# Seven half-block products in place of eight: three quarters of each MLP's second product by Strassen's scheme

## Chip, cores and metric

One core of a Trainium2 chip runs the whole kernel as one program. The metric is the device time of one execution in microseconds. The engines are named as the profile names them: PE is TensorE's matmul, DVE is VectorE, ACT is ScalarE, POOL is GpSimd, SP is the engine whose queue issues the DMAs.

## What is computed

The reference is a two-layer encoder on 512 tokens of width 1024, all in float32: layer 0 has windowed and neighbourhood attention, layer 1 a bidirectional state-space scan. Each layer ends in the same MLP with a squared relu:

```python
def squared_relu_mlp(x, w1, w2):
    return jnp.square(jax.nn.relu(x @ w1)) @ w2
...
x = layer_norm(DN_ALPHA * x + mix, ln1_g[i], ln1_b[i])
x = layer_norm(DN_ALPHA * x + squared_relu_mlp(x, mlp_w1[i], mlp_w2[i]), ln2_g[i], ln2_b[i])
```

`w1` is 1024 x 4096 and `w2` is 4096 x 1024. The change touches the product with `w2`.

## The kernel before

Every large product is done with operands split in two: `hi` is the value rounded to the matmul's fp32r type, `lo` the rest, and `split3` (line 215) adds three matmuls, hi x hi, hi x lo and lo x hi. A full matmul has 512 columns and contracts 128 rows.

**Weights.** `Weights` (line 42) walks a list of chunks of 128 x 1024 values in the order of their use. `prepare` loads a chunk by SP (line 73, tile `w_raw`), makes `w_hi` on ACT (line 74) and `w_lo` on DVE, or on POOL for the chunks that `ON_POOL` lists (line 75). `next` keeps three chunks ahead of the one that it returns. The pool "w" has four buffers of each tile; `widen` (line 84) adds a second pool "w2" with four more, and then four chunks in turn come from "w2" and four from "w".

**The MLP** (`Main.mlp`, line 416) works in four quarters of 1024 hidden values. In a quarter the first product makes eight tiles of 128 hidden values x 512 tokens (`project`, 24 matmuls a chunk), and `act` makes relu and square on ACT, the square again in fp32 and its low half on DVE. The second product (`sweep`, line 281) goes over two halves of 512 output columns. In each, eight k-tiles meet four groups of 128 tokens, in four PSUM banks: 4 chunks x 24 matmuls. So a quarter has 192 + 192 matmuls. `drain` (line 321) adds a bank to the residual rows `res` on DVE. The last quarter's second half is followed by the layer norm and by transposes; the first quarter's first four tiles run as half-width pieces (`first_tiles`).

**Order.** PE's order is as written; in the MLP quarters the instructions of ACT, DVE, POOL and SP are ordered by a scheduler when the program is built, and each engine then works strictly in that order.

Of the kernel before, what the change touches and what calls it, by code (L numbers as in the profile page):

```python
# [9 lines left out]
F32 = mybir.dt.float32  # L10
# [17 lines left out]
G = 8  # L28
# [13 lines left out]
class Weights:  # L42


    def __init__(self, nc, pool, sources, ahead, in_order):
        self.in_order = in_order
        self.nc = nc
        self.pools = [pool]
# [4 lines left out]
        self.wide_from = self.wide_until = 0  # L53
        self.at = 0

    def prepare(self, after=(), between=None):
# [3 lines left out]
        src = self.sources[self.at]  # L60
        wide = self.wide_from <= self.at < self.wide_until and (self.at - self.wide_from) % (4 + self.extra) < self.extra
        pool = self.pools[1 if wide else 0]
        self.at += 1
        n = src.shape[1]
        raw = pool.tile([P, 1024], F32, name="w_raw")
# [5 lines left out]
        eng = nc.gpsimd if self.at - 1 in ON_POOL else nc.vector  # L71
        for cols in (slice(0, n),) if between is None else (slice(0, n // 2), slice(n // 2, n)):
            nc.sync.dma_start(out=raw[:, cols], in_=src[:, cols])
# [9 lines left out]

    def widen(self, pool, extra, n):


        self.extra = extra
        self.pools = [self.pools[0], pool]
        self.wide_from = self.at + 4 - len(self.ready)
        self.wide_until = self.at - len(self.ready) + n  # L90
# [28 lines left out]
def tile_encoder_trunk(ctx: ExitStack, tc: tile.TileContext, a: dict, out: bass.AP, stop=None):  # L119
# [36 lines left out]
    for q in range(4):  # L156
        sources += [a["w_m1"][0, q * 8 + i] for i in range(8)]
        sources += [a["w_m2"][0, q, i] for i in range(8)]
    sources += [a["w_dt"]]
    sources += [a["w_ssm"][i] for i in range(6 * G)]  # L160
    sources += [a["w_so"][i] for i in range(16)]
    for q in range(4):
        sources += [a["w_m1"][1, q * 8 + i] for i in range(8)]
        sources += [a["w_m2"][1, q, i] for i in range(8)]
# [92 lines left out]
    class Main:  # L257
# [10 lines left out]
        def more_weights(self, bufs, n):  # L268
            self.w2_ctx = tc.tile_pool(name="w2", bufs=bufs)
            weights.widen(self.w2_ctx.__enter__(), bufs, n)  # L270

        def fewer_weights(self):
            self.w2_ctx.__exit__(None, None, None)

# [141 lines left out]
        def mlp(self, layer, ends):  # L416
            xh, xl = rows_of(self.xT[0]), rows_of(self.xT[1])
            hh, hl = rows_of(self.h_slots.hi()), rows_of(self.h_slots.lo())
# [9 lines left out]
            for q in range(4):  # L428
                first = 0
                if q == 0:  # L430
                    first = 4
                    for i, ps in enumerate(self.first_tiles(first)):
                        act(ps, i)
                for i in range(first, 8):
                    ps = mm_bank()
                    project(ps, weights.next(), xh, xl)
                    act(ps, i)
                if q == 3:
                    self.load_ln(2 * layer + 1)
# [959 lines left out]
```

## Time and profile before

| | us |
|---|---|
| median of three runs | 1416.11 (1415.49 to 1420.14) |
| the profiled execution | 1418.63 |
| its span, first to last instruction | 1416.8 |
| PE busy | 1386.0 (98%) |
| DVE busy | 837.8 (59%) |
| ACT busy | 619.6 (44%) |
| POOL busy | 356.5 (25%) |

The page gives for each engine the time in which an instruction of it was in work. A time in which an instruction of DVE or POOL is held up after it has started counts as busy too. Matmuls are pipelined, so their busy times overlap and pace is read from their starts, or from what each finished tile releases.

### The profile page before, as it was taken

How to read it: one execution, taken by the hardware profiler on the slowest of the kernel's cores; microseconds unless marked ns; L12 is line 12 of the kernel's file. 1: busy time of each engine (PE TensorE's matmuls, PEld its weight loads, DVE VectorE, ACT ScalarE, POOL GpSimd, SP SyncE). 2: the span in 40 equal slices, each digit the busy share in tenths (PEclk: the TensorE clock that was granted, in tenths of full speed). 3: DMA queues.
4: the chain of work that ended last, by engine and by line, in shares of the span. 5: the costliest groups of instructions: out<-in, count | busy, mean ns of one | idle time of the engine just before them, and what ended most of it. 6: DMA issues, size and time to landing. Idle time of an engine off the chain costs nothing.

```text
span 1416.8 us, 18694 instructions
## 1 busy us (share of the span) xinstructions
PE 1386.0 (98%) x7104; PEld 1142.2 (81%) x7104; DVE 837.8 (59%) x1222; ACT 619.6 (44%) x1105; POOL 356.5 (25%) x248
## 2 busy tenths in 40 slices
PE   8999999999999999998999999999999999999997
PEld 7777779888888888986888788878888888888886
DVE  4577559434344343869789788887586243443426
ACT  5688725314133140357766567664324133231320
POOL 1255310000000020216664657665213000000000
PEclk9999999999999999999999999999999999999999
DMA  8232255333333230245454454532544233232101
GB/s 295 79 124 64 68 196 176 105 93 101 90 105 90 86 100 30 100 129 154 144 151 132 132 154 145 156 101 77 198 152 161 77 110 98 89 104 75 60 0 60
DMA packets 62401, 161.48 MB, mean 114 GB/s; under 512 B 9612, under 2 KB 19624, under 8 KB 62312
## 3 DMA queue, kind: packets, MB, share of 16 engines
q1 hardware_dynamic: 62312, 160.29, 36.4%
q8 instruction: 56, 0.92, 0.3%
q14 instruction: 33, 0.27, 0.1%
HBM read 154.87 MB, written 5.39 MB: 113 GB/s over the span
## 4 chain that ended last, share of the span: by engine, by line
PE 81%; DVE 6%; POOL 4%; DMA 3%; issue 2%; ACT 1%; SPq 1%; DVEq 0%; POOLq 0%; ACTq 0%
PE mm L216 19%; PE mm L217 19%; PE mm L218 19%; PE b L217 5%; PE b L218 5%; PE b L216 5%; POOL tb L947 1%; POOL e L956 1%; DVE xs L843 1%; PE y L1099 1%; SPq L548 1%; DVE w_lo L75 1%; PE y L1110 1%; PE o L635 1%; DMA r<-ac_d 1%
## 5 line engine op out<-in xcount | busy, mean ns | idle before, releaser
L74 ACT ACTIVATE w_hi<-w_raw 128x1024 fp32r<-128x1024 f32 (+1 forms) x216 | 225.8, 1052 | 462.7 <-PE mm L217 201.8
L216 PE MATMUL mm<-hi,w_hi 128*128 128x512 f32 (+1 forms) x1048 | 412.9, 394 | 0.0
L75 DVE TENSOR_TENSOR w_lo<-w_raw,w_hi 128x1024 fp32r<-128x1024 f32 (+1 forms) x185 | 254.0, 1377 | 252.3 <-ACT w_hi L74 251.5
L217 PE MATMUL mm<-lo,w_hi 128*128 128x512 f32 (+1 forms) x1048 | 398.5, 380 | 0.0
L218 PE MATMUL mm<-hi,w_lo 128*128 128x512 f32 (+1 forms) x1048 | 397.4, 379 | 0.0
L216 PEld LDWEIGHTS mm<-hi,w_hi 128*128 128x128 f32 x1048 | 197.1, 188 | 40.4 <-issue 5.5
L218 PEld LDWEIGHTS mm<-hi,w_lo 128*128 128x128 f32 x1048 | 196.9, 188 | 39.2
L217 PEld LDWEIGHTS mm<-lo,w_hi 128*128 128x128 f32 x1048 | 197.6, 189 | 33.0
L75 POOL TENSOR_TENSOR w_lo<-w_raw,w_hi 128x1024 fp32r<-128x1024 f32 (+1 forms) x31 | 76.7, 2479 | 411.5 <-ACT w_hi L74 411.5
L216 PE MATMUL mm<-w_hi,hi 128*128 128x512 f32 x352 | 141.2, 401 | 5.7 <-ACT hi L178 5.0
L218 PE MATMUL mm<-w_hi,lo 128*128 128x512 f32 x352 | 138.9, 394 | 0.0
L217 PE MATMUL mm<-w_lo,hi 128*128 128x512 f32 x352 | 138.8, 394 | 0.0
L217 PE MATMUL b<-w_lo,hi 128*128 128x512 f32 (+1 forms) x328 | 123.5, 377 | 1.6 <-DVE w_lo L75 1.6
L216 PE MATMUL b<-w_hi,hi 128*128 128x512 f32 (+1 forms) x328 | 123.6, 377 | 0.0
L218 PE MATMUL b<-w_hi,lo 128*128 128x512 f32 (+1 forms) x328 | 123.4, 376 | 0.0
L370 POOL TENSOR_TENSOR rstd<-ve,half 128x1 f32<-128x1 f32 x16 | 13.1, 819 | 358.8 <-DVE neg L368 339.6
L947 POOL TENSOR_TENSOR tb<-r,dmask 128x1024 f32<-128x1024 f32 x32 | 83.7, 2626 | 31.3 <-DMA r<-ac_d 30.1
L951 ACT ACTIVATE tb<-tb,ac_tok 128x128 f32<-128x128 f32 x256 | 80.6, 390 | 22.5 <-POOL tb L947 22.5
L216 PEld LDWEIGHTS mm<-w_hi,hi 128*128 128x128 f32 x352 | 66.7, 189 | 20.9 <-ACT hi L178 5.0
L218 PEld LDWEIGHTS mm<-w_hi,lo 128*128 128x128 f32 x352 | 66.5, 189 | 15.5 <-DVE lo L239 0.4
L217 PEld LDWEIGHTS mm<-w_lo,hi 128*128 128x128 f32 x352 | 66.7, 189 | 13.8
L425 DVE TENSOR_TENSOR sq<-relu 128x512 f32<-128x512 f32 x64 | 60.5, 948 | 24.4 <-ACT relu L423 24.4
(287 smaller groups left out, 1883.8 us busy)
## 6 DMA issues: line engine op xcount, KB each, us to landing
w_raw<-in_w_m_dram SPq DMA_DIRECT2D x128, 512.0 KB, 3.6
w_raw<-in_w_ssm_dram SPq DMA_DIRECT2D x48, 512.0 KB, 3.6
r<-ac_d SPq DMA_DIRECT2D x64, 256.0 KB, 4.6
w_raw<-in_w_so_dram SPq DMA_DIRECT2D x16, 512.0 KB, 3.7
w_raw<-in_w_att_dram SPq DMA_DIRECT2D x14, 512.0 KB, 5.8
r<-ac_d SPq DMA_DIRECT2D x64, 96.0 KB, 2.9
w_raw<-in_w_ao_dram SPq DMA_DIRECT2D x8, 512.0 KB, 3.6
xraw<-in_xT_dram SPq DMA_DIRECT2D x8, 256.0 KB, 6.4
```

The costliest lines, as they stand in the source:

```text
L74: split = [nc.scalar.activation(hi[:, cols], raw[:, cols], AF.Copy), eng.tensor_tensor(lo[:, cols], raw[:, cols], hi[:, cols].bitcast(F32) ...
L75: eng.tensor_tensor(lo[:, cols], raw[:, cols], hi[:, cols].bitcast(F32), op=ALU.subtract)]
L216: PE.matmul(ps, lhs_h, rhs_h, start=first, stop=False)
L217: PE.matmul(ps, lhs_h, rhs_l, start=False, stop=False)
L218: PE.matmul(ps, lhs_l, rhs_h, start=False, stop=last)
L425: DVE.tensor_tensor(s, r, r, op=ALU.mult)
L548: nc.sync.dma_start(out=vj[r * 32:r * 32 + 32, j, kt, :], in_=vb_g[kt * 4 + r, NA_START[j]:NA_START[j] + 32, pair * P:pair * P + P])
L635: PE.matmul(o_ps[64 * e:64 * e + 64, self.n * P:self.n * P + P], va[:, b, kv:kv + 64], self.pt[e][:, i * P:i * P + P], start=(i == 0), sto ...
L843: DVE.scalar_tensor_tensor(acc[:, lo_o:lo_o + n], ps[:, lo_i:lo_i + n], cw[:, i, k:k + 1], acc[:, lo_o:lo_o + n], op0=ALU.mult, op1=ALU.add)
L947: POOL.tensor_tensor(v["x"], v["r"].rearrange("p d (c l) -> p d c l", c=NT), bc(dmask.unsqueeze(2), [P, 2, NT, P]), op=ALU.add)
L951: pin(ACT.activation(v["x"][:, d, c, :], v["x"][:, d, c, :], AF.Exp, bias=ac_tok[:, c, 32 * d + hf:32 * d + hf + 1]))
L956: POOL.tensor_tensor(es[g, h], v["x"][:, 0], v["x"][:, 1], op=ALU.add)
```

## The change

In the quarters 0, 1 and 2 of both layers the second product is done by blocks. The quarter's hidden values are a 2 x 2 block matrix H (512 tokens as two halves of 256, 1024 hidden values as two halves of 512), the weights a 2 x 2 block matrix W of 512 x 512 blocks. Seven products of block sums replace the eight products of blocks. Each has 24 matmuls in two PSUM banks.

- Sums of H blocks are made by DVE in the fp32 tile `s` and split again into four slots of the `hi` and `lo` tiles.
- Sums of W blocks are made by POOL (`less`), in fp32, in the eight raw tiles `w2r` of a quarter and two tiles `t1`. The chunk list then has 14 entries for such a quarter; of their low halves DVE makes eleven, POOL those of the entries 7, 10 and 13.
- One product goes into two places of `res` (two pairs of DVE additions from PSUM). One product is copied by ACT to `u`; two others are added to it by DVE, and POOL adds `u` to `res`.
- `w_raw` has three buffers instead of four. The pool "w2" holds raw blocks and is no longer a source of `w_hi` and `w_lo`, save for four chunks at a time that are lent at the ends of two sweeps of layer 0.

```diff
-        raw = pool.tile([P, 1024], F32, name="w_raw")
+        made = callable(src)
+        raw = src() if made else pool.tile([P, 1024], F32, name="w_raw", bufs=3)
...
-        eng = nc.gpsimd if self.at - 1 in ON_POOL else nc.vector
+        eng = nc.gpsimd if on_pool else nc.vector
...
+        def less(to, x, y, p):
+            nc.gpsimd.tensor_tensor(v[to, p], v[x, p], v[y, p], op=ALU.subtract)
+        def get(b, p, *sums):
+            def make():
+                if not v:
+                    for i, name in enumerate(("11", "21", "12", "22")):
+                        for j in range(2):
+                            v[name, j] = blocks["pool"].tile([P, 1024], F32, name="w2r")
+                            nc.sync.dma_start(out=v[name, j], in_=a["w_m2"][layer, q, 2 * i + j])
+                    for j in range(2):
+                        v["T1", j] = blocks["pool"].tile([P, 1024], F32, name="t1", bufs=2)
+                        less("T1", "12", "11", j)
+                        less("12", "22", "12", j)
+                for args in sums:
+                    less(*args, p)
+                return v[b, p]
+            return make
+        for b, *sums in (("11",), ("21", ("11", "22", "T1")), ("T1", ("21", "21", "11")), ("22",), ("11",), ("12",), ("21",)):
+            chunks += [get(b, p, *sums) for p in range(2)]
...
+                sources.extend((c, i in (7, 10, 13)) for i, c in enumerate(sums))
...
+        def act(self, ps, i):
...
+            if i in (5, 7):
...
+                DVE.tensor_tensor(h22, h21, h22, op=ALU.add)
+                DVE.tensor_tensor(h21, h11, h21, op=ALU.subtract)
+                DVE.tensor_tensor(h11, h22, h11, op=ALU.subtract)
+                DVE.tensor_tensor(h12, h12, h11, op=ALU.subtract)
+            if i == 7:
+                self.split(3, self.s[:, 1, :, 256:])
...
+        def product(self, o):
+            banks = [mm_bank() for _ in range(2)]
+            for p in range(2):
+                wh, wl = weights.next()
+                for kk in range(2):
+                    k = 2 * p + kk
+                    for t in range(2):
+                        ts = slice(t * P, t * P + P)
+                        cs = slice(kk * 512, kk * 512 + 512)
+                        split3(banks[t], self.hi[:, o, k, ts], self.lo[:, o, k, ts], wh[:, cs], wl[:, cs],
+                               k == 0, k == 3)
...
+        def products(self, scale):
+            x = self.product(0)
+            self.split(0, s[:, 1, :, :256])
+            for t in range(2):
+                ACT.activation(u[t], x[t], AF.Copy)
+            self.add(x, 0, 0, scale)
+            x = self.product(1)
+            self.split(1, s[:, 0, :, :256])
+            self.add(x, 0, 0)
+            x = self.product(3)
+            self.split(3, s[:, 0, :, 256:])
+            self.add(x, 1, 1, scale)
+            self.add(x, 0, 1, scale)
+            self.add(self.product(0), 0, 1)
+            x = self.product(1)
+            for t in range(2):
+                DVE.tensor_tensor(u[t], u[t], x[t], op=ALU.add)
+            self.add_u(u, 0, 1)
+            x = self.product(3)
...
+            self.add_u(u, 1, 1)
+            self.add(self.product(2), 1, 0, scale)
+            self.add_u(u, 1, 0)
```

The built orders show what this moves. DVE in the second product of layer 0's first quarter, before (`w_lo` is a chunk's low half, `res` with `mm` or `b` an addition from PSUM), and now, from chunk 4 (`t1`) to the activation splits of the slots 0 and 1 (`lo<-s,hi`; `s<-s` are sums):

```order
L75 TENSOR_TENSOR w_lo_3250<-w_raw_3248,w_hi_3249 128x1024
L75 TENSOR_TENSOR w_lo_3281<-w_raw_3279,w_hi_3280 128x1024
L75 TENSOR_TENSOR w_lo_3312<-w_raw_3310,w_hi_3311 128x1024
L323 SCALAR_TENSOR_TENSOR res0_2383<-res0_2383,mm_3085 128x512
L323 SCALAR_TENSOR_TENSOR res1_2384<-res1_2384,mm_3086 128x512
L323 SCALAR_TENSOR_TENSOR res2_2385<-res2_2385,mm_3087 128x512
L323 SCALAR_TENSOR_TENSOR res3_2386<-res3_2386,mm_3088 128x512
L75 TENSOR_TENSOR w_lo_3343<-w_raw_3341,w_hi_3342 128x1024
```

```order
L75 TENSOR_TENSOR w_lo_3131<-t1_2990,w_hi_3130 128x1024
L534 TENSOR_TENSOR s_2672<-s_2672 128x2x256
L278 TENSOR_TENSOR lo_2674<-s_2672,hi_2673 128x1024
L370 SCALAR_TENSOR_TENSOR res0_2383<-res0_2383,mm_3110 128x512
L535 TENSOR_TENSOR s_2672<-s_2672 128x2x256
L370 SCALAR_TENSOR_TENSOR res1_2384<-res1_2384,mm_3111 128x512
L75 TENSOR_TENSOR w_lo_3156<-t1_2993,w_hi_3155 128x1024
L536 TENSOR_TENSOR s_2672<-s_2672 128x2x256
L75 TENSOR_TENSOR w_lo_3172<-w2r_2986,w_hi_3171 128x1024
L372 TENSOR_TENSOR res0_2383<-res0_2383,mm_3152 128x512
L372 TENSOR_TENSOR res1_2384<-res1_2384,mm_3153 128x512
L278 TENSOR_TENSOR lo_2674<-s_2672,hi_2673 128x1024 x2
```

The splits of block sums and the additions of each product now alternate with the weight splits, where eight additions stood in two groups.

POOL after layer 0's first layer norm, before, and now at the end of the first quarter's second product, from chunk 7 to chunk 13 (`t1` is a block sum of the next quarter, `res` with `sq` the addition of `u`):

```order
L370 TENSOR_TENSOR rstd_2654<-ve_2651,half_75 128x1
L75 TENSOR_TENSOR w_lo_3529<-w_raw_3527,w_hi_3528 128x1024
L75 TENSOR_TENSOR w_lo_4522<-w_raw_4520,w_hi_4521 128x1024
L75 TENSOR_TENSOR w_lo_4633<-w_raw_4631,w_hi_4632 128x1024
L75 TENSOR_TENSOR w_lo_4781<-w_raw_4779,w_hi_4780 128x1024
```

```order
L75 TENSOR_TENSOR w_lo_3194<-w2r_2988,w_hi_3193 128x1024
L75 TENSOR_TENSOR w_lo_3250<-w2r_2982,w_hi_3249 128x1024
L162 TENSOR_TENSOR t1_3587<-w2r_3579,w2r_3571 128x1024
L563 TENSOR_TENSOR res0_2383<-res0_2383,sq_3108 128x512
L162 TENSOR_TENSOR t1_3590<-w2r_3581,w2r_3573 128x1024
L563 TENSOR_TENSOR res1_2384<-res1_2384,sq_3109 128x512
L75 TENSOR_TENSOR w_lo_3308<-w2r_2980,w_hi_3307 128x1024
```

POOL had six full splits in the whole MLP of layer 0. Now two block sums of the next quarter and two additions stand ahead of chunk 13's split.

SP at the same place, before, and now (the blocks of the second quarter; `w2r_3577` takes the buffer of chunk 9, `w2r_3579` that of chunk 10, `w2r_3581` that of chunk 11):

```order
L73 DMA w_raw_3217<-in_w_m2_dram 128x1024
L73 DMA w_raw_3248<-in_w_m1_dram 128x1024
L73 DMA w_raw_3279<-in_w_m1_dram 128x1024
L73 DMA w_raw_3310<-in_w_m1_dram 128x1024
L73 DMA w_raw_3341<-in_w_m1_dram 128x1024
```

```order
L170 DMA w2r_3575<-in_w_m2_dram 128x1024
L170 DMA w2r_3577<-in_w_m2_dram 128x1024
L170 DMA w2r_3579<-in_w_m2_dram 128x1024
L170 DMA w2r_3581<-in_w_m2_dram 128x1024
L170 DMA w2r_3583<-in_w_m2_dram 128x1024
L73 DMA w_raw_3391<-in_w_m1_dram 128x1024
L73 DMA w_raw_3427<-in_w_m1_dram 128x1024
L170 DMA w2r_3585<-in_w_m2_dram 128x1024
```

The loads of the next quarter's blocks stand in one run, each behind the release of a buffer by this quarter's splits.

## Rows read from the trace of the kernel before

**Rows 1.** The page: busy time, share of the span, instructions.
```profile
PE 1386.0 (98%) x7104; PEld 1142.2 (81%) x7104; DVE 837.8 (59%) x1222; ACT 619.6 (44%) x1105; POOL 356.5 (25%) x248
```

**Rows 2.** Windows, layer 0's third quarter: us, then busy per engine, PEclk, DMA.
```profile
core 0: us, PE busy (x) PEld busy (x) DVE busy (x) ACT busy (x) POOL busy (x), PEclk, DMA share, GB/s
408.60:497.10 88.50, 88.50 (x385) 72.16 (x385) 35.00 (x39) 25.95 (x33) 2.40 (x1) 1.00 0.31 94
```

**Rows 3.** Timeline of ACT in that quarter: start us, us, instruction [idle before <-releaser].
```profile
408.67 0.58 ACT L423 ACTIVATE relu<-mm 128x512 f32<-128x512 f32 x1
414.27 0.58 ACT L423 ACTIVATE relu<-mm 128x512 f32<-128x512 f32 x1
...
430.95 0.58 ACT L423 ACTIVATE relu<-mm 128x512 f32<-128x512 f32 x1
...
436.39 0.58 ACT L423 ACTIVATE relu<-mm 128x512 f32<-128x512 f32 x1
...
457.77 1.06 ACT L74 ACTIVATE w_hi<-w_raw 128x1024 fp32r<-128x1024 f32 x1 [4.57 <-PE mm L218]
463.39 1.06 ACT L74 ACTIVATE w_hi<-w_raw 128x1024 fp32r<-128x1024 f32 x1 [4.56 <-PE mm L218]
```

**Rows 4.** Timelines of DVE and POOL: durations of undisturbed operations.
```profile
1061.49 2.41 DVE L75 TENSOR_TENSOR w_lo<-w_raw,w_hi 128x1024 fp32r<-128x1024 f32 x2 [0.54 <-ACT w_hi L74]
...
1079.26 1.29 DVE L426 TENSOR_TENSOR lo<-sq,hi 128x512 fp32r<-128x512 f32 x2
...
1118.40 2.05 DVE L323 SCALAR_TENSOR_TENSOR res<-res,mm 128x512 f32<-128x512 f32 x3 [1.08 <-PE mm L218]
...
695.87 1.29 POOL L956 TENSOR_TENSOR e<-tb 128x512 f32<-128x512 f32 x1
...
519.59 2.40 POOL L75 TENSOR_TENSOR w_lo<-w_raw,w_hi 128x1024 fp32r<-128x1024 f32 x1 [19.81 <-ACT w_hi L74]
```

**Rows 5.** The same timelines where DVE and POOL have work at once.
```profile
515.20 0.68 DVE L425 TENSOR_TENSOR sq<-relu 128x512 f32<-128x512 f32 x1
...
520.03 2.50 DVE L425 TENSOR_TENSOR sq<-relu 128x512 f32<-128x512 f32 x1 [3.34 <-ACT relu L423]
...
580.13 5.72 POOL L75 TENSOR_TENSOR w_lo<-w_raw,w_hi 128x1024 fp32r<-128x1024 f32 x2 [2.24 <-ACT w_hi L74]
...
583.51 0.41 DVE L325 TENSOR_TENSOR res<-res,b 128x256 f32<-128x256 f32 x1
...
690.47 3.45 POOL L947 TENSOR_TENSOR tb<-r,dmask 128x1024 f32<-128x1024 f32 x1
...
690.47 4.54 DVE L75 TENSOR_TENSOR w_lo<-w_raw,w_hi 128x1024 fp32r<-128x1024 f32 x2
...
693.88 2.03 POOL L1166 TENSOR_TENSOR pv<-pv,cdec 128x512 f32<-128x512 f32 x1
```

**Rows 6.** The page, DMA issues: what, count, KB each, us to landing.
```profile
w_raw<-in_w_m_dram SPq DMA_DIRECT2D x128, 512.0 KB, 3.6
```

**Rows 7.** Windows in the scan of layer 1, columns as in rows 2.
```profile
660.00:664.00 4.00, 0.58 (x11) 0.51 (x12) 3.90 (x4) 3.64 (x7) 2.42 (x1) 1.00 0.84 213
664.00:668.00 4.00, 4.00 (x23) 3.10 (x20) 2.10 (x3) 1.57 (x2) 2.24 (x2) 0.57 0.45 130
...
944.00:948.00 4.00, 3.28 (x19) 2.48 (x18) 3.57 (x4) 1.32 (x3) 4.00 (x3) 1.00 0.47 131
948.00:952.00 4.00, 3.12 (x14) 2.21 (x13) 3.05 (x3) 3.98 (x7) 1.83 (x1) 1.00 0.00 0
```

**Rows 8.** Timelines of SP and ACT in the attention stage.
```profile
35.20 15.00 SPq L548 DMA_DIRECT2D vj<-vb_d  x32
50.30 0.84 SPq L73 DMA_DIRECT2D w_raw<-in_w_att_dram  x2
53.90 1.06 ACT L74 ACTIVATE w_hi<-w_raw 128x1024 fp32r<-128x1024 f32 x1 [2.40 <-DMA w_raw<-in_w_att_dram]
```

More of the change, by code (lines that the diff above doesn't have):

```diff
@@ L47, in __init__ @@
         self.nc = nc
-        self.pools = [pool]
+        self.pool = pool
         self.ahead = ahead
@@ L59, in prepare @@
         nc = self.nc
-        src = self.sources[self.at]
-        wide = self.wide_from <= self.at < self.wide_until and (self.at - self.wide_from) % (4 + self.extra) < self.extra
-        pool = self.pools[1 if wide else 0]
+        src, on_pool = self.sources[self.at]
+        pool = self.pool
         self.at += 1
-        n = src.shape[1]
-        raw = pool.tile([P, 1024], F32, name="w_raw")
+        made = callable(src)
+        raw = src() if made else pool.tile([P, 1024], F32, name="w_raw", bufs=3)
+        n = 1024 if made else src.shape[1]
         if self.lent:
@@ L155, in tile_encoder_trunk, with tag @@
     sources += [a["w_ao"][i] for i in range(8)]
[L156 to L164, printed above, removed]
+    blocks = {}
+    def tag(chunks):
+        tagged = [(c, len(sources) + i - made[0] in ON_POOL) for i, c in enumerate(chunks)]
+        return tagged
@@ new lines, in block_sums @@
+    def block_sums(layer, q):
+        v = {}
+        def less(to, x, y, p):
[15 more added lines that the diff above has]
+            return make
+        chunks = []
+        for b, *sums in (("11",), ("21", ("11", "22", "T1")), ("T1", ("21", "21", "11")), ("22",), ("11",), ("12",), ("21",)):
+            chunks += [get(b, p, *sums) for p in range(2)]
+        return chunks
@@ new lines, in tile_encoder_trunk, with add_mlp @@
+    made = [0]
+    def add_mlp(layer):
+        for q in range(4):
+            sources.extend(tag([a["w_m1"][layer, q * 8 + i] for i in range(8)]))
+            if q < 3:
+                sums = block_sums(layer, q)
+                sources.extend((c, i in (7, 10, 13)) for i, c in enumerate(sums))
+                made[0] += len(sums) - 8
+            else:
+                sources.extend(tag([a["w_m2"][layer, q, i] for i in range(8)]))
+    sources[:] = [(c, i in ON_POOL) for i, c in enumerate(sources)]
@@ L165, in tile_encoder_trunk @@
+    add_mlp(0)
+    rest = [a["w_dt"]]
+    rest += [a["w_ssm"][i] for i in range(6 * G)]
+    rest += [a["w_so"][i] for i in range(16)]
+    sources.extend(tag(rest))
+    add_mlp(1)
     weights = Weights(nc, w_pool, sources, 3, in_order)
@@ L266, in __init__, with open_blocks, close_blocks, lend @@
                 nc.sync.dma_start(out=self.res[t], in_=load_from[t * P:(t + 1) * P, :])
[L268 to L272, printed above, removed]
+        def open_blocks(self):
+            self.w2_ctx = tc.tile_pool(name="w2", bufs=8)
+            self.w2 = blocks["pool"] = self.w2_ctx.__enter__()
+            self.s_ctx = tc.tile_pool(name="sq_all", bufs=1)
+            self.s_pool = self.s_ctx.__enter__()
+        def close_blocks(self):
+            self.s_ctx.__exit__(None, None, None)
             self.w2_ctx.__exit__(None, None, None)
+        def lend(self):
+            t = [self.w2.tile([P, 1024], F32R, name="w2r") for _ in range(8)]
+            return [(t[2 * i], t[2 * i + 1]) for i in range(4)]
         def load_ln(self, row):
@@ L428, in mlp @@
             for q in range(4):
+                if q < 3:
+                    blocked = Blocked(self)
+                    take = blocked.act
+                else:
+                    hh, hl = rows_of(self.h_slots.hi()), rows_of(self.h_slots.lo())
+                    take = act
                 first = 0
@@ L436, in mlp @@
                     project(ps, weights.next(), xh, xl)
-                    act(ps, i)
-                if q == 3:
-                    self.load_ln(2 * layer + 1)
-                self.sweep(hh, hl, q == 0, **(ends if q == 3 else {}))
+                    take(ps, i)
+                if q < 3:
+                    blocked.products(q == 0)
+                    continue
+                self.load_ln(2 * layer + 1)
+                self.sweep(hh, hl, False, **ends)
         def overlapped(self, then=None):
```

68 lines of the change are left out of this document (47 added, 21 removed).

## The prediction

> **What bounds the kernel now.** I read the page first, then the MLP stages by windows, then single engines in time. TensorE (PE) is busy for nearly the whole span, while VectorE (DVE), ScalarE (ACT) and GpSimd (POOL) are far from it [rows 1]. One quarter of an MLP, the third of layer 0, shows the same without a gap: 88.50 us, all of them PE, with 385 recorded matmuls where the program has 384, POOL nearly idle, DVE at 35.00 [rows 2]. So a matmul taken away there is worth its own time, until another engine can no longer keep up.
>
> The pace has two levels. The relu of each chunk marks the end of its 24 matmuls: the first chunks of the quarter are 5.60 us apart, the later ones 5.44, and the first chunks of the second product 5.62 [rows 3]. That is 233 to 234 ns a matmul against 226.7. The steps change every four chunks, as the pools do from which the weight halves come: four chunks from the extra pool "w2" (slow), four from the pool "w" (fast). About half of the MLP's chunk steps are slow.
>
> **What leaves PE.** A half-block product is 24 matmuls (two 128-token groups, four k, three terms). Seven instead of eight take 24 from each of six quarters: 144 matmuls; the built program has exactly these fewer on PE, so the change does what it says. And after it all matmul weights of the quarters come from "w", where every row so far is fast. A Strassen quarter then takes (192 + 168) x 0.2267 = 81.6 us, 6.9 less than the 88.50. Four quarters (the second and third of each layer) give 4 x 6.9 = 27.6. The first quarter's first four chunks run in half-width pieces that I leave as they are; its second product goes from 96 x 0.234 + 96 x 0.2267 = 44.2 to 38.1: 2 x 6.1 = 12.2. The last quarter keeps its matmuls, and eight of its chunks change pace: 192 x 7 ns = 1.3, twice 2.6. Sum: **42.4 us less**, if nobody is late.
>
> The Trainium skill, page "TensorE: Matmul & The Clock Gate", section "Wait — 56ns, not 53.3ns?", gives 215.7 ns for back-to-back matmuls of 512 columns at the full clock, one pace; by it the 144 would be an estimated 31.1 us and no second pace would exist to win. The rows have two paces, both above it, so I take theirs; the page's rule comes back as a rival.
>
> **What is added, and where.** Durations: a DVE operation on 1024 elements takes 1.2 us in a row of two, one on 512 with both inputs in SBUF 0.65, an addition from PSUM 0.7; on POOL 2.4 for 1024 and 1.3 for 512 [rows 4]; ACT 1.06 and 0.6 [rows 3]. DVE and POOL do not run beside each other freely: a DVE square that alone takes 0.68 took 2.50 while POOL had its 2.40, and ended after it; an addition from PSUM ran in 0.41 inside a POOL stretch, unharmed. When both have work they alternate: POOL's 1024 took 3.45, DVE's two splits 4.54, POOL's next 2.03 [rows 5]. So each POOL operation costs DVE its length, unless DVE is then idle or on PSUM.
>
> Per Strassen quarter the second product has, on DVE, eleven weight splits, four activation splits (15 x 1.2 = 18), the last square, lo and sums (6 x 0.65 = 3.9) and fourteen PSUM additions (9.8): 31.7 us of 38.1. POOL has, in the same stretch and in the quarters that another Strassen quarter follows, six operations of 2.4 and two of 1.3: 17.0. Together 48.7 in 38.1, so at least 10.6 us of POOL must fall beside PSUM additions (9.8) or in DVE's idle 6.4. That is possible only with perfect packing, and the orders are fixed. In the first product there is room: DVE has some 20 us of work (eight splits, sixteen shorter operations, four of the sums), POOL up to 20, in 43.5. ACT needs some 36 of 82 us, and a quarter still loads sixteen chunks; both are hidden.
>
> *First late place: the fourth product.* It reads block sum h11 (slot 0). Its matmuls start at 3 x 5.44 = 16.3 us after the second product began, and want the low half 0.23 later. DVE can start on that stretch at 1.1, when ACT's first weight half is there. It then does four weight splits (4.8), two activation splits (2.4), six 512s (3.9) and four PSUM additions (2.8): 13.9, so 15.0 unblocked. Two POOL operations fall inside: block sum "21" (2.4), started as soon as the fourth weight chunk is split, and chunk 7's split, released by ACT 2.1 us after the last activation sum, just ahead of DVE's slot-0 split: 2.0 of it not beside additions. 19.4 against 16.5: **2.9 late**. One bank wait before it (DVE's second addition is 0.3 after the third product wants it): 3.2 per quarter. Bounds: 0 if POOL's sum comes after DVE's stretch, 5 if one more POOL operation falls in.
>
> *Second late place: chunk 13, the last half of the seventh product.* DVE goes on from 19.4: slot 1 split, chunk 8, four additions, slot 3 split, chunk 9, in all 7.6, plus 0.8 behind POOL's chunk 10: 27.8. PE begins chunk 9 at 27.7 with the lateness so far, and would want chunk 13's low half at 38.8. But POOL's chunk 13 stands behind the two first block sums of the next quarter. The first of these waits for a load that SP issues only after one that waits for chunk 9's split (the buffers are the same eight). A load lands 3.6 us after its issue [rows 6], with two issues of 0.4 [rows 8]: 32.2. Then sum, addition, sum, addition, split: 2.4 + 1.3 + 2.4 + 1.3 + 2.4 = 9.8, ending at 42.0, or 44.4 with two DVE splits let in between. **3.2 to 5.6 late; I take 5.0, since both splits are due there**, in the four quarters that a Strassen quarter follows. Lower bound 0: chunk 9 split 3 us earlier. Upper 7: the two loads land one behind the other. Behind the late chunk only the next first product is queued, which has 16 us of slack.
>
> *The clock.* After 3.4 us without a matmul the granted clock was 0.57 over the next 4 us, that is the lower of the two levels (1.2 instead of 2.4 GHz) for 3.4 us: 1.7 us lost. Two gaps of about 0.8 each did not lower it [rows 7]. So 1.7 for each of the four long waits, 6.8; nothing for the 2.9 ones, which lie between (at most 1.7 each, 10).
>
> *Elsewhere.* With three raw buffers in place of four, the seventh attention chunk's load moves behind 32 small ones on SP (15.0 us), and ACT's split of it now stands in front of the q that PE waits for; that split waited for its load already [rows 8]. One more split and its load: 1.5 (0 to 3).
>
> **Sum:** -42.4 + 6 x 3.2 + 4 x 5.0 + 6.8 + 1.5 = +5.1. Against the profiled execution's 1418.6 that is 1423.7; it stood 2.5 above the median of the three runs, so **1421 us**. Its own range: 1411 to 1431.
>
> **Rivals.**
> - *DVE and POOL find room* (the other side, faster). One mechanism: POOL's operations fall beside PSUM additions and in DVE's pauses. For it: 16.2 us of such time per quarter and POOL's 17.0 are nearly equal, and each PE wait gives DVE time. Against: the fixed order. It decides at chunk 13: with chunk 9 split some 3 us earlier the last chunk is 1 late instead of 5 and the clock holds. Then -42.4 + 6 x 2 + 4 x 2 + 1.5 = -21, **1395 us**; with no stall at all 1375.
> - *The second pace is not the pool's.* The Trainium skill, page "SBUF — State Buffer", section "Who interferes with whom", says that PE never waits on anyone for SBUF; by that rule the place of the weights can't set the pace. As a mechanism here: the slow steps follow the alternation by chunk number and stay. About 1,400 matmuls keep 7 ns: 9.8 us more, **1431**. Against it: the step falls from 5.60 to 5.44 at the fourth chunk, where the pool changes, and rises again where it changes back.
> - *The clock falls at all ten late places.* Six more losses of 1.7, and each late operation itself a little later: **1436**. For it: 2.9 us is nearer to the gap that lowered the clock than to those that did not. Against: no row shows a single gap of that length.
>
> **Chances.** Forecast 0.48, room 0.32, pace 0.10, clock 0.10. Three runs of this kernel spread by 0.3%, so less than that can't be told from no change: 1411.9 to 1420.4. Faster: 0.28 from room and 0.08 from the forecast's lower part, 0.36. Same: 0.20. Slower: 0.44. The range 1390 to 1434 leaves out the best of the second case (0.09) and the worst of the last two (0.09).
>
> **What would show it.** PE with 6,960 matmuls; chunk steps at 5.44 everywhere in the quarters (if 5.6 remains: the pace rival). At each fourth product a PE wait of about 3 us on DVE's activation split; at the seventh products of the first two quarters of each layer 5 us on POOL's weight split, with the clock lower behind it. POOL's block sum there should start at a load's landing. If these waits are under 1 us, my count of blocked time is wrong and the kernel is faster. If the fourth product waits much longer, DVE is simply too full.

## The result: 0.8% slower

| | before | after |
|---|---|---|
| median, 5 runs each | 1418.78 (1415.49 to 1420.14) | 1428.22 (1425.61 to 1429.75) |
| ratio, 95% interval | | 1.0077 (1.0065 to 1.009) |
| profiled span | 1416.8 | 1426.2 |
| mean granted clock | 0.993 | 0.982 |

The forecast was 1421, 5.1 us more than before; measured were 9.4 more, in the medians as in the spans. All times below are microseconds of the profiled executions unless they are called medians.

### The profile page after: what moved, and what is told of

The parts are those of the page before. It is cut to its first block, busy times and chain, and to the rows that moved or that the text cites. A ratio compares the mean times of both kernels' runs of the same rounds, so it can differ in the third digit from the quotient of the medians.

```text
span 1426.2 us, 18843 instructions
## 1 busy us (share of the span) xinstructions
PE 1364.4 (96%) x6960; PEld 1123.1 (79%) x6960; DVE 1023.0 (72%) x1365; ACT 681.9 (48%) x1177; POOL 589.6 (41%) x345
## 4 chain that ended last, share of the span: by engine, by line
PE 66%; DVE 10%; POOL 9%; issue 6%; DMA 5%; ACT 2%; SPq 1%; DVEq 0%; POOLq 0%; ACTq 0%
PE mm L255 17%; PE mm L257 17%; PE mm L256 17%; POOL w_lo L75 3%; DVE w_lo L75 2%; PE b L257 2%; PE b L255 2%; PE b L256 2%; POOL tb L1088 1%; POOL e L1097 1%; DMA r<-ac_d 1%; DVE lo L278 1%; PE y L1240 1%; DVE lo L528 1%; SPq L689 1%
## 5 line engine op out<-in xcount | busy, mean ns | idle before, releaser
L255 PE MATMUL mm<-hi,w_hi 128*128 128x512 f32 x920 | 375.4, 408 | 0.0
L257 PE MATMUL mm<-hi,w_lo 128*128 128x512 f32 x920 | 361.5, 393 | 2.4 <-POOL w_lo L75 2.4
L256 PE MATMUL mm<-lo,w_hi 128*128 128x512 f32 x920 | 360.5, 392 | 0.0
L75 DVE TENSOR_TENSOR w_lo<-w_raw,w_hi 128x1024 fp32r<-128x1024 f32 (+1 forms) x137 | 221.4, 1621 | 145.9 <-ACT w_hi L74 145.6
L256 PE MATMUL mm<-w_lo,hi 128*128 128x512 f32 x496 | 200.1, 403 | 15.3 <-POOL w_lo L75 14.0
L255 PE MATMUL mm<-w_hi,hi 128*128 128x512 f32 x496 | 202.9, 409 | 9.9 <-ACT hi L217 4.8
L257 PE MATMUL mm<-w_hi,lo 128*128 128x512 f32 x496 | 199.8, 403 | 11.6 <-DVE lo L278 10.1
L74 ACT ACTIVATE w_hi<-w2r 128x1024 fp32r<-128x1024 f32 x72 | 76.1, 1057 | 135.0 <-PE mm L256 74.9
L75 POOL TENSOR_TENSOR w_lo<-w_raw,w_hi 128x1024 fp32r<-128x1024 f32 x23 | 57.0, 2480 | 90.1 <-ACT w_hi L74 84.7
L75 DVE TENSOR_TENSOR w_lo<-w2r,w_hi 128x1024 fp32r<-128x1024 f32 x54 | 70.8, 1313 | 30.8 <-ACT w_hi L74 30.8
L75 POOL TENSOR_TENSOR w_lo<-w2r,w_hi 128x1024 fp32r<-128x1024 f32 x18 | 55.2, 3068 | 88.1 <-ACT w_hi L74 88.1
L162 POOL TENSOR_TENSOR w2r<-w2r 128x1024 f32<-128x1024 f32 x24 | 68.2, 2841 | 39.3 <-DVE w_lo L75 25.5
L528 DVE TENSOR_TENSOR lo<-s,hi 128x256 fp32r<-128x256 f32 (+1 forms) x48 | 77.1, 1609 | 4.5
```

Of the source, the lines that this page charges most:

```text
L74: split = [nc.scalar.activation(hi[:, cols], raw[:, cols], AF.Copy), eng.tensor_tensor(lo[:, cols], raw[:, cols], hi[:, cols].bitcast(F32) ...
L75: eng.tensor_tensor(lo[:, cols], raw[:, cols], hi[:, cols].bitcast(F32), op=ALU.subtract)]
L162: nc.gpsimd.tensor_tensor(v[to, p], v[x, p], v[y, p], op=ALU.subtract)
L255: PE.matmul(ps, lhs_h, rhs_h, start=first, stop=False)
L256: PE.matmul(ps, lhs_h, rhs_l, start=False, stop=False)
L257: PE.matmul(ps, lhs_l, rhs_h, start=False, stop=last)
```

## The profile after, beside the rows of before

The page, busy time and instructions, against [rows 1]:

```profile
PE 1364.4 (96%) x6960; PEld 1123.1 (79%) x6960; DVE 1023.0 (72%) x1365; ACT 681.9 (48%) x1177; POOL 589.6 (41%) x345
```

PE has the 144 matmuls fewer, DVE and POOL are over 180 and 230 us busier, and PE now stands still. The view of waits for PE says for whom (engine, line, releaser: us in total, times, longest):

```profile
PE mm L256 <- POOL w_lo L75: 14.0, 4, 5.3
PE mm L257 <- DVE lo L278: 10.1, 6, 1.9
...
PE mm L255 <- DVE res L370: 3.2, 2, 3.0
...
PE mm L257 <- POOL w_lo L75: 2.4, 1, 2.4
...
PE mm L257 <- DVE lo L528: 1.5, 1, 1.5
```

These are the two late places of the prediction (L278 is the split of a slot, L75 on POOL that of chunk 13) and some more, which stand in layer 0's first quarter (L370, L528) and behind a chunk 13 (2.4).

**The pace.** ACT's relus in layer 0's third quarter, against [rows 3]:

```profile
418.75 0.58 ACT L520 ACTIVATE relu<-mm 128x512 f32<-128x512 f32 x1
424.19 0.58 ACT L520 ACTIVATE relu<-mm 128x512 f32<-128x512 f32 x1
...
435.07 0.58 ACT L520 ACTIVATE relu<-mm 128x512 f32<-128x512 f32 x1
440.51 0.58 ACT L520 ACTIVATE relu<-mm 128x512 f32<-128x512 f32 x1
```

All seven steps of the quarter are 5.44; no step of 5.60 is left in any quarter.

**The fourth product**, layer 0's second quarter. PE, DVE and POOL in time (start, us, instruction, [idle before <-releaser]):

```profile
383.73 0.39 PE L256 MATMUL mm<-w_lo,hi 128*128 128x512 f32 x1
385.97 0.50 PE L257 MATMUL mm<-w_hi,lo 128*128 128x512 f32 x1 [1.85 <-DVE lo L278]
```
```profile
370.44 2.70 DVE L528 TENSOR_TENSOR lo<-s,hi 128x512 fp32r<-128x512 f32 x1
...
375.52 1.22 DVE L278 TENSOR_TENSOR lo<-s,hi 128x1024 fp32r<-128x1024 f32 x1
...
382.52 3.39 DVE L278 TENSOR_TENSOR lo<-s,hi 128x1024 fp32r<-128x1024 f32 x2
385.84 1.21 DVE L75 TENSOR_TENSOR w_lo<-w2r,w_hi 128x1024 fp32r<-128x1024 f32 x1
```
```profile
369.87 2.72 POOL L162 TENSOR_TENSOR w2r<-w2r 128x1024 f32<-128x1024 f32 x1 [1.82 <-issue]
380.14 3.55 POOL L75 TENSOR_TENSOR w_lo<-w2r,w_hi 128x1024 fp32r<-128x1024 f32 x1 [7.55 <-ACT w_hi L74]
```

PE goes on when the pair of DVE splits that began at 382.52 is done. Beside POOL's sum of "21" (369.87) a DVE operation of 0.65 took 2.70, and beside POOL's chunk 7 (380.14) two splits of 1.2 took 3.39. It is the blocking of [rows 5].

**Chunk 13**, same quarter. SP's loads of the next quarter's blocks, and POOL:

```profile
381.49 16.80 SPq L170 DMA_DIRECT2D w2r<-in_w_m_dram  x7
```
```profile
398.14 2.41 POOL L162 TENSOR_TENSOR t<-w2r 128x1024 f32<-128x1024 f32 x1 [4.15 <-DMA w2r<-in_w_m_dram]
400.49 1.30 POOL L563 TENSOR_TENSOR res<-res,sq 128x512 f32<-128x512 f32 x1
401.73 2.42 POOL L162 TENSOR_TENSOR t<-w2r 128x1024 f32<-128x1024 f32 x1
404.07 2.31 POOL L563 TENSOR_TENSOR res<-res,sq 128x512 f32<-128x512 f32 x1
406.35 3.32 POOL L75 TENSOR_TENSOR w_lo<-w2r,w_hi 128x1024 fp32r<-128x1024 f32 x1
```
```profile
409.72 0.50 PE L256 MATMUL mm<-w_lo,hi 128*128 128x512 f32 x1 [3.04 <-POOL w_lo L75]
```

The chain is the one forecast: the first sum begins when a load lands, and then come sum, addition, sum, addition, split. The matmul that reads this split waits 3.04 for it.

**The clock** in the same quarter; PE stands still from 384.1 to 386.0 and from 406.7 to 409.7, and the window behind shows the granted clock (columns as in rows 2, PEclk third from the end):

```profile
384.00:388.00 4.00, 2.15 (x9) 1.63 (x9) 4.00 (x5) 1.53 (x2) 0.00 (x0) 0.92 0.50 173
388.00:392.00 4.00, 4.00 (x13) 3.21 (x12) 3.71 (x5) 1.06 (x1) 1.40 (x1) 0.65 0.42 131
404.00:408.00 4.00, 2.68 (x12) 1.88 (x10) 4.00 (x5) 1.89 (x2) 4.00 (x3) 1.00 0.41 111
408.00:412.00 4.00, 2.28 (x10) 1.89 (x11) 2.88 (x3) 0.00 (x0) 4.00 (x2) 1.00 0.79 190
412.00:416.00 4.00, 4.00 (x20) 3.29 (x19) 2.90 (x3) 1.06 (x1) 4.00 (x3) 1.00 0.63 227
```

The clock fell after the gap of 2.2 us (0.65 over the next four) and not after the one of 3.4 (gaps are from one matmul's start to the next one's). In all it fell at nine places of the quarters, each time 6 to 9 matmuls at 0.43 in place of 0.227: some 65 matmuls by 0.2, 13 us. Five of the nine stand behind fourth products (not in layer 0's first quarter), two behind a late chunk 13, one behind the chunk after a chunk 13, and one behind a bank wait in layer 0's first quarter.

**The whole by stages.** The marks are the starts of the first relu of each quarter (of the fourth one in layer 0's first quarter); layer 0's fourth quarter ends at the first relu of layer 1's scan stage, and layer 1's first second product runs from the eighth relu of its quarter. So the difference can be put beside the working of the prediction:

| stage | before | after | difference | forecast |
|---|---|---|---|---|
| start to fourth relu of layer 0 | 248.7 | 246.1 | -2.6 | +1.5 |
| rest of first quarter | 71.5 | 83.1 | +11.6 | +3.8 |
| second quarter | 88.5 | 89.6 | +1.1 | +3.0 |
| third quarter | 88.5 | 86.2 | -2.2 | -3.7 |
| fourth quarter | 100.9 | 99.6 | -1.3 | -1.3 |
| to layer 1's first second product | 501.4 | 500.4 | -1.0 | 0 |
| that product | 49.8 | 54.8 | +5.0 | +3.8 |
| second quarter | 88.4 | 91.6 | +3.2 | +3.0 |
| third quarter | 88.5 | 86.3 | -2.2 | -3.7 |
| rest | 90.8 | 88.6 | -2.2 | -1.3 |
| sum | 1416.8 | 1426.2 | +9.4 | +5.1 |

Eight of the ten stages lie within 2 us of the forecast. The one that is off by most, layer 0's first quarter, has a cause that the prediction did not look at. Its raw blocks are loaded into buffers that have been lent out at the end of the sweep before, and hold the weights of the quarter's first four chunks: SP issues the eight loads in pairs between 237.3 and 246.4, each pair behind the matmul that read the buffers last, and POOL waits for them:

```profile
250.86 5.74 POOL L162 TENSOR_TENSOR t<-w2r 128x1024 f32<-128x1024 f32 x2 [24.33 <-DMA w2r<-in_w_m_dram]
256.56 2.85 POOL L162 TENSOR_TENSOR w2r<-w2r 128x1024 f32<-128x1024 f32 x1
259.37 2.85 POOL L162 TENSOR_TENSOR w2r<-w2r,t 128x1024 f32<-128x1024 f32 x1
```
```profile
252.42 1.92 DVE L75 TENSOR_TENSOR w_lo<-w2r,w_hi 128x1024 fp32r<-128x1024 f32 x1 [4.48 <-ACT w_hi L74]
254.26 2.89 DVE L521 TENSOR_TENSOR s<-relu 128x512 f32<-128x512 f32 x1
257.25 2.71 DVE L528 TENSOR_TENSOR lo<-s,hi 128x512 fp32r<-128x512 f32 x1
259.88 3.41 DVE L75 TENSOR_TENSOR w_lo<-w2r,w_hi 128x1024 fp32r<-128x1024 f32 x1
```

Six sums in a row, 250.86 to 268.4, each of which costs a DVE operation about 2 us: DVE enters the second product late, PE waits 1.3 on a weight split, 1.5 on a square's low half and 3.0 on a bank, where the clock falls, then 0.9 at the fourth product.

## The experiments

The theory: everything that took the 42.4 us back is POOL's block sums, by two ways: beside DVE's work (fourth product) and ahead of chunk 13 on POOL's own queue; and the pace comes from the place of the weights. The rivals: DVE is too full by itself, and the pace goes by chunk number. Added lines move the line numbers of a kernel's rows by up to 9.

### The pace alone

The kernel before, all MLP weights from the pool "w":

```diff
             self.w2_ctx = tc.tile_pool(name="w2", bufs=bufs)
-            weights.widen(self.w2_ctx.__enter__(), bufs, n)
+            self.w2 = self.w2_ctx.__enter__()
+            if bufs == 1:
+                weights.widen(self.w2, bufs, n)
...
-            main.sweep(yh, yl, True, begun=begun, **main.overlapped())
+            main.sweep(yh, yl, True, begun=begun, lend=main.lend, **main.overlapped())
```

> The kernel before, eight products, with all MLP weight halves from the pool w; the extra pool only lends four pairs to the two finishing sweeps of layer 0, as the changed kernel does. Pace theory (the pool, that is the place in SBUF, sets the pace): the chunk steps of 5.60 us in the quarters become 5.44 everywhere; 8 slow steps per quarter go, about 1,400 matmuls by 7 ns, 9.8 us, and with the 2.6 us that the changed kernel gained ahead of its first MLP quarter the span falls from 1416.8 to about 1404. Rival (the pace goes by chunk number, not by place): 5.60 stays at the same chunks and the span is 1414 to 1417. Rival (the second set of buffers was needed): 5.44 steps, but waits on weight splits take back 3 us or more.

Measured: median 1405.84, ratio 0.9914 (0.9887 to 0.994), span 1405.4. ACT's relus in layer 0's second quarter:

```profile
319.06 0.58 ACT L429 ACTIVATE relu<-mm 128x512 f32<-128x512 f32 x1
...
324.50 0.58 ACT L429 ACTIVATE relu<-mm 128x512 f32<-128x512 f32 x1
```

The steps are 5.44 at every chunk, and the time is the forecast 1404 within 1.5. The rival by chunk number falls. The second set of buffers was not needed.

Is it the pool or the place? The same pool at other addresses, in layer 0 alone:

```diff
         def __init__(self, stack, li, load_from, x_slots, h_slots):
             self.x_slots, self.h_slots = x_slots, h_slots
+            if li == 0:
+                self.w2_ctx = tc.tile_pool(name="w2", bufs=4)
+                self.w2 = stack.enter_context(self.w2_ctx)
             self.res_pool = stack.enter_context(tc.tile_pool(name=f"res{li}", bufs=1))
```

> The kernel before, with the extra weight pool of layer 0 opened ahead of the residual and the other tiles of that stage, so that its halves w_hi and w_lo begin at bytes 154,464 and 170,848 of a partition in place of 192,000 and 208,384; layer 1 is left as it was, and the order of the work too. If the place in SBUF sets the pace: the chunk steps of 5.60 us in the quarters of layer 0 become 5.44, those of layer 1 stay, and the span falls by about 4.5 us. If it is the alternation of the pools or the chunk number: 5.60 stays in both layers.

Measured in a single execution: 1411.52 against a median of 1417.03 for the kernel before, span 1409.8. Relus of layer 0's second quarter, and of a stretch in layer 1:

```profile
319.21 0.58 ACT L426 ACTIVATE relu<-mm 128x512 f32<-128x512 f32 x1
...
324.65 0.58 ACT L426 ACTIVATE relu<-mm 128x512 f32<-128x512 f32 x1
...
1165.09 0.58 ACT L426 ACTIVATE relu<-mm 128x512 f32<-128x512 f32 x1
...
1170.69 0.58 ACT L426 ACTIVATE relu<-mm 128x512 f32<-128x512 f32 x1
```

5.44 in layer 0, where the pool has moved, 5.60 in layer 1, where it hasn't. The alternation of the pools is the same in both layers, so it is not the cause; the layout is. The edit also moves the residual and the other tiles of the stage, which now lie behind the pool. The run before left those tiles where they were and had 5.44 with the pool "w" alone, so the one cause that fits both runs is the place of the weights; this is argued, no run shows it by itself.

### The block sums left out

The kernel leaves out the 48 subtractions of weight blocks; only its time is of use.

```diff
         def less(to, x, y, p):
-            nc.gpsimd.tensor_tensor(v[to, p], v[x, p], v[y, p], op=ALU.subtract)
+            return
...
-                        v["T1", j] = blocks["pool"].tile([P, 1024], F32, name="t1", bufs=2)
+                        v["T1", j] = v["12", j]
```

> The changed kernel without the block sums of the weights: the 48 subtractions on GpSimd are left out, so the products use blocks as they are. Theory (all the late places come from these sums beside VectorE's work and ahead of chunk 13): all waits over 0.5 us in the quarters go, with the clock's falls, and the span is about 1380. Rival (VectorE's own 31.7 us in 38.1 and the fixed order make at least the fourth product late): 1395 to 1410, with waits of 1 us or more at the fourth products and the clock lower behind them.

Measured: median 1373.53, ratio 0.9683 (0.9663 to 0.9704), span 1371.8. In PE's waits there is no line for a weight split, and of L278 only

```profile
PE mm L257 <- DVE lo L278: 1.5, 2, 0.7
```

Without the sums the clock falls nowhere in the quarters, and the span is 8 us below the 1380 expected. The 54.4 us between this span and 1426.2 hang on 48 operations of POOL that PE never waits for directly. DVE, with its own splits and POOL's of chunks 7, 10 and 13 beside them, keeps up: that rival falls.

### Chunk 13 ahead of the next quarter's sums

```diff
-            nc.gpsimd.tensor_tensor(v[to, p], v[x, p], v[y, p], op=ALU.subtract)
+            ins = nc.gpsimd.tensor_tensor(v[to, p], v[x, p], v[y, p], op=ALU.subtract)
+            if to == "T1" and weights.on_pool is not None:
+                in_order(ins, weights.on_pool)
```

(`on_pool` is POOL's latest weight split of such a quarter.)

> The changed kernel, with the first block sums of the next quarter ordered on GpSimd behind its split of chunk 13. Queue theory: TensorE's four waits on that split (14.0 us), the 2.4 us one behind them and the three falls of the clock after them (about 1.6 each) go, 1426 becomes about 1406 in the span; TensorE has no gap over 1 us at the seventh products. Rival (GpSimd and VectorE are simply full there): the split of chunk 13 is still late by 2 us or more, or the sums are now late for the next quarter's second product, and the span stays within 5 us of 1426. The fourth products keep their waits of about 2 us under both.

Measured: median 1404.19, ratio 0.9904 (0.9878 to 0.993), span 1402.0. POOL in the second quarter:

```profile
392.75 2.41 POOL L76 TENSOR_TENSOR w_lo<-w2r,w_hi 128x1024 fp32r<-128x1024 f32 x1
395.11 6.74 POOL L165 TENSOR_TENSOR t<-w2r 128x1024 f32<-128x1024 f32 x2
```

The split comes first and PE has no gap at the seventh products. One new wait, 3.9 on a weight split of layer 1's next first product, now stands behind the sums. The fourth products keep their gaps of 2.2 us, as foreseen. But of the five after the first quarter only one lowered the clock here, where all five did in the changed kernel: three falls in the quarters in place of nine. So of the 24.2 us gained 14.0 are the waits at chunk 13, and some 9 are clock (20 slow matmuls in place of some 65), most of it at fourth products, which the order of work was not meant to touch.

### The fourth product

First the sum "21" moved behind POOL's splits of chunks 7 and 10:

```diff
-("T1", ("21", "21", "11")), ("22",), ("11",), ("12",), ("21",)):
+("T1",), ("22",), ("11",), ("12", ("21", "21", "11")), ("21",)):
...
+            if to == "21" and weights.on_pool is not None:
+                in_order(ins, weights.on_pool)
```

> The changed kernel, with block sum 21 (two operations) ordered on GpSimd behind its splits of chunks 7 and 10 instead of standing ahead of the fourth product; the second sum T1 moves behind chunk 13 with it. Theory (that sum holds VectorE up ahead of the fourth product by 2.4 us or more): the six waits of 1.9 us at the fourth products, the bank waits ahead of them (3.2 us in all) and the six falls of the clock that follow (1.6 each) go, some 20 us, span about 1406; the waits at chunk 13 stay or shrink. Rival (VectorE is too full there by itself): a wait of 1.5 us or more stays at each fourth product, span 1418 to 1430. Rival (the moved sums now delay chunks 8 to 12): new waits there, span above 1420.

Measured: median 1425.89, ratio 1.0057 (1.0041 to 1.0072), span 1419.9. The range, 1421.78 to 1428.1, overlaps that of the changed kernel. The waits did not go, they grew:

```profile
PE mm L262 <- DVE lo L283: 18.5, 6, 4.0
```

DVE and POOL in the second quarter:

```profile
371.80 6.72 DVE L283 TENSOR_TENSOR lo<-s,hi 128x1024 fp32r<-128x1024 f32 x2
```
```profile
371.71 2.42 POOL L76 TENSOR_TENSOR w_lo<-w2r,w_hi 128x1024 fp32r<-128x1024 f32 x1 [18.72 <-ACT w_hi L75]
374.07 3.36 POOL L165 TENSOR_TENSOR w2r<-w2r 128x1024 f32<-128x1024 f32 x1
```

DVE begins its pair of splits 3.5 us ahead of the matmul at which PE stops (375.27), in the changed kernel 1.2 ahead, but it now meets two POOL operations instead of one, and one split is let in between them. So the theory had the wrong operation: what holds PE here is whatever POOL does beside that pair. Then why a pair? In program order slot 0, which the fourth product reads, is split first; but slot 0 takes the last of DVE's four sums (L536, block h12) and slot 1 the one before it (L535, h11). ACT in the trace splits slot 1 first, and the scheduler put DVE's split of slot 1 first too. That can be turned round alone:

```diff
-            self.split(0, s[:, 1, :, :256])
+            early = self.split(0, s[:, 1, :, :256])
...
-            self.split(1, s[:, 0, :, :256])
+            in_order(self.split(1, s[:, 0, :, :256]), early)
```

> The changed kernel with one order on VectorE turned round: the split of slot 0, which the fourth product reads, ahead of that of slot 1, which only the fifth reads. If the fourth product waits for both splits in a row: its six waits shrink from 1.9 by one split, 1.2 us, to about 0.7, 7 us less in all, and if the clock then no longer falls there another 10, span 1409 to 1419. If the split of slot 0 is itself held behind GpSimd's split of chunk 7: the wait stays at 1.9 or above, span within 3 us of 1426.

Measured: median 1425.71, ratio 1.0057 (1.0035 to 1.0078), span 1420.6. The fourth product, and chunk 13 of the same quarter:

```profile
381.81 0.39 PE L256 MATMUL mm<-w_lo,hi 128*128 128x512 f32 x1
382.89 0.50 PE L257 MATMUL mm<-w_hi,lo 128*128 128x512 f32 x1 [0.69 <-DVE lo L278]
...
402.14 0.39 PE L255 MATMUL mm<-w_hi,hi 128*128 128x512 f32 x1
407.84 0.79 PE L256 MATMUL mm<-w_lo,hi 128*128 128x512 f32 x1 [5.31 <-POOL w_lo L75]
```

The wait fell from 1.85 to 0.69, as expected for one split, and after none of the five gaps of 1.1 did the clock fall. Yet only 5.6 us came in the spans and 2.5 in the medians, whose ranges overlap, where 7 to 17 were forecast: the waits at chunk 13 rose from 14.0 to 20.1, since PE came earlier to a split that was no earlier. A wait removed ahead of a later one is worth only what the later one leaves.

### The changes together

All of it: T1 behind chunk 13, slot 0 first, both sums of "21" behind chunk 10, and layer 1's first products with DVE's splits alone.

> The changed kernel with four orders changed: the sums T1 behind chunk 13 (as in e3), block sum 21 behind chunk 10 on GpSimd, slot 0 ahead of slot 1 on VectorE, and the weight splits of layer 1's first products all on VectorE. Theory: against e3 (span 1402.0) the fourth products lose most of their 2.2 us and the clock's fall of some 1.6 behind each, and the 4.3 us gap of layer 1 goes: 1402 - 13 - 9 - 5 = about 1376. Rival (the later sums hold the next quarter's loads, and with them the first product's weights on the same queue): new waits at chunks of the first products, span above 1392.

Measured: median 1397.46, ratio 0.9861 (0.9839 to 0.9882), span 1394.2. The fourth products are free, but there is a gap of 2.8 in each of six quarters, on a weight split of DVE (14.6 us of PE's waits). Neither case of the expectation came: the time is above the rival's 1392, but the new waits are not at the first products. The next kernel keeps that order and makes the first quarter plain again:

```diff
-            if q < 3:
+            if q < 3 and layer + q > 0:
                 sums = block_sums(layer, q)
```

> As e7_all_orders, and layer 0's first quarter again by eight products, so that its blocks are not needed while their buffers are still lent out. That puts 24 matmuls back, 5.4 us, and takes away the waits of that quarter, 8.1 us in e3 and some 3 of clock behind them. If e7 has still those waits, this one is about 5 us below it; if the orders of e7 have cleared them, it is 5 us above.

Measured: median 1394.59, ratio 0.9841 (0.9817 to 0.9865), span 1393.0; 2.9 in the median and 1.2 in the span below the one before, where the two cases were 5 below or 5 above; the ranges of the two kernels overlap. DVE, PE and POOL at the new gap:

```profile
378.16 3.38 DVE L76 TENSOR_TENSOR w_lo<-w2r,w_hi 128x1024 fp32r<-128x1024 f32 x1
```
```profile
381.59 0.50 PE L261 MATMUL mm<-w_lo,hi 128*128 128x512 f32 x1 [2.43 <-DVE w_lo L76]
```
```profile
377.12 6.67 POOL L165 TENSOR_TENSOR w2r<-w2r 128x1024 f32<-128x1024 f32 x2
```

The two sums now sit on DVE's split of chunk 9. I took it for chunk 12 and put one of them back ahead of chunk 10:

> As e8_plain_first_quarter, with the two operations of block sum 21 one behind chunk 7 and one behind chunk 10 on GpSimd (as in e4) in place of both behind chunk 10. If the 2.8 us gaps of e8 at chunk 12 come from the first of them standing behind chunk 10: the five gaps and the falls of the clock behind three of them (some 1.6 each) go, 1393.0 - 14 - 5 = about 1374, and since slot 0 is split ahead of slot 1 the fourth products don't wait either. If that sum holds slot 0's split up (as slot 1's and 0's in e4): gaps of 1 to 3 us at the fourth products and a span of 1380 to 1393.

> As e10_sum21_split_up, with layer 0's first quarter by seven products again (all six quarters, as in the changed kernel). Its blocks land only when the lent buffers come back, so its waits of 2.9 us and more stay in that quarter, and with the clock they outweigh the 5.4 us of matmuls saved: e10 plus 2 to 5 us. If the moved sums clear that quarter too: e10 less 3 to 5.

Measured: 1395.6, ratio 0.9848 (0.9832 to 0.9863), and 1399.03, ratio 0.9869 (0.9852 to 0.9887). The first expectation missed: gaps of 0.8 (a bank, at the fifth product) and 2.3 (the split of chunk 9) stand in every blocked quarter. The second agrees with the medians, 3.4 above, but the spans are equal (1397.5 and 1397.0) and the ranges overlap. At both places tried between the fourth product and chunk 12, POOL's operations fall on the DVE split that PE needs next or on one ahead of it in DVE's queue. So I changed not the order but the amount:

```diff
-            ins = nc.gpsimd.tensor_tensor(v[to, p], v[x, p], v[y, p], op=ALU.subtract)
+            eng = nc.vector if to == "21" else nc.gpsimd
+            ins = eng.tensor_tensor(v[to, p], v[x, p], v[y, p], op=ALU.subtract)
...
-                sources.extend((c, i in (7, 10, 13)) for i, c in enumerate(sums))
+                sources.extend((c, i == 13) for i, c in enumerate(sums))
```

> As e10_sum21_split_up, with the two operations of block sum 21 and the splits of chunks 7 and 10 moved from GpSimd to VectorE (the sums ordered behind the split of slot 0); GpSimd keeps chunk 13, T1 and the rest. Theory (where the two engines alternate, a GpSimd operation costs VectorE its 2.4 us, and the same work on VectorE itself 1.2): the second product's joint work falls by four times 1.2, more than the 2.3 to 2.8 us gaps that wandered from chunk to chunk in e7, e8 and e10; they go, with the clock, 1397 to about 1375, and no gap over 1 us is left in the quarters. Rival (VectorE alone is now too full, 36.5 us and the additions in 38.1): the gap moves once more, 1.5 us or more in each quarter, span above 1388.

> As e12_sums_on_dve, with seven products in layer 0's first quarter too. 5.4 us of matmuls less; its waits there were 5.7 us and more in e11, with a fall of the clock. If moving the 4 operations clears half of them: within 3 us of e12, on either side; if they stay whole: 2 to 5 us above; if they go: 5 us below, about 1370.

Measured: **1379.82**, ratio 0.974 (0.9727 to 0.9754), span 1377.1 where about 1375 was expected, and 1379.95, ratio 0.9742 (0.9729 to 0.9756). DVE in the second quarter of the first of the two:

```profile
367.67 2.35 DVE L286 TENSOR_TENSOR lo<-s,hi 128x1024 fp32r<-128x1024 f32 x2
369.94 2.35 DVE L166 TENSOR_TENSOR w2r<-w2r 128x1024 f32<-128x1024 f32 x2
372.21 1.22 DVE L76 TENSOR_TENSOR w_lo<-w2r,w_hi 128x1024 fp32r<-128x1024 f32 x1
```

All at their undisturbed lengths, with POOL idle until chunk 13. PE has no gap over 1 us in any quarter, and the clock does not fall there. From the last relu of that quarter to the first of the next are 43.92 us, against 43.52 for eight steps of 5.44. This version beats both kernels: 2.6% under the one before. Of this, 0.9% is had with eight products already (the first experiment); the five blocked quarters give the rest, 28.3 us between the spans 1405.4 and 1377.1, where 120 matmuls by 0.2267 are 27.2. With all six quarters blocked the first keeps a gap of 2.8, slow matmuls behind it and a second bank wait, 5.8 us in all, which eat the 5.4 us of matmuls; no difference between the two can be measured.

## Why the prediction was right, point by point

The mechanisms of the two late places were right, and they are most of what took the gain back. That the total missed by only 4.3 us is in part luck: by stages it is 7.8 too little for layer 0's first quarter against 4.1 too much ahead of it, and the rest comes to 0.6.

- **What leaves PE: right.** 6,960 matmuls, 5.44 everywhere. The kernel without sums has a median of 1373.5; the prediction's case without any stall was 1375. The rival "the second pace is not the pool's" falls by two runs. The Trainium skill, page "SBUF — State Buffer", section "Who interferes with whom", says that PE never waits on anyone. It speaks of one engine waiting for another, not of where a tile lies, so the prediction drew more from it than it states; here a matmul took 226.7 or 233 to 234 ns by the layout, and the measurement decides.
- **The fourth product: mechanism right, sizes off that nearly cancel.** 2.9 and 0.3 for the bank were forecast; measured were 1.9 and 0.2 in five quarters, and 0.9 and 3.0 in layer 0's first. The end of slot 0's split was forecast 19.4 us after the second product began, and in layer 0's second quarter it came at 18.9. The prediction took slot 0 for h11; it is h12, one sum later, and so the scheduler puts the split of slot 1, which was left out, ahead of it (1.2). DVE began 0.4 later than counted. Against that, 4.4 us of blocking were taken where some 3.1 came (2.05 beside the sum, about 1.0 beside chunk 7), and DVE's other operations were 0.8 shorter.
- **Chunk 13: right in mechanism, smaller in size.** 20 forecast; 14.0 measured, and 2.4 at the chunk behind it. I took 5.0 for each of the four, and they came out between 2 and 5.3. The run with the other order shows that the place in POOL's queue caused it.
- **The clock: this step failed.** I took 6.8 for the four late chunks 13 and nothing for the fourth products; it fell at nine places, five of them fourth products and only two a chunk 13, and cost some 13 us. The rival "the clock falls at all ten late places" was the better guess of where, with seven of its ten, though its 1436 assumed the waits at full size. In the rows a gap of 2.2 us lowers the clock in one kernel and mostly not in another, 3.4 us once did not, 1.1 never did. What else decides it is not settled.
- **The attention stage: wrong.** The late split of the seventh chunk was there (53.46, in place of 46.77), but of the 1.5 forecast only 0.5 came: PE was 0.3 ahead of the kernel before and then 0.2 behind it. The stage was shorter in the end: a wait of 1.6 on a weight split near 201 us is gone. What moved that split I did not test.
- **Layer 0's first quarter: missed**, 7.8 us. The prediction priced it like layer 1's first quarter and did not ask when its blocks' buffers come free.
- **"DVE and POOL find room": wrong for this order, and it needed more than a shift in time.** Three orders of the same POOL work only moved the gap; fewer POOL operations in the second product removed it. The run that did so also gave the sums "21" a new place, behind the split of slot 0; amount and place were not tried apart.

## What to carry to other kernels

When DVE operations with both inputs in SBUF and POOL operations meet, they alternate; count a POOL operation there at its own length against DVE, and compare that with DVE doing it itself (here 2.4 against 1.2). Look first at what an engine's queue does ahead of the late instruction, and expect that a wait removed early in a stretch can be met again later in it, as here until the amount of work fell. Before paying for an algorithm with fewer products, look at the pace of the products themselves: here taking the extra weight buffers out of use gave 0.9% with no new work.

## What was not expected of the hardware

- The layout of SBUF, most likely the place of the weights, sets the pace of the matmuls: in layer 0, 226.7 ns with the extra pool's `w_hi` from byte 154,464 of a partition and its `w_lo` from 170,848, and with the pool "w"; 233 to 234 with the extra pool from 192,000 and 208,384. These bytes are the program's layout as it was put on record with the run; the profile shows none. Where the step lies and why is open.
- The clock does not follow the length of a gap alone: five gaps of 2.2 us lowered it in the changed kernel, and of five equal gaps in the kernel with chunk 13 first only one did.
